# First layer's moba queries computed with queries along the free axis, in four accumulators, with the rotary step on GpSimd

## The chip, the cores and the metric

The kernel runs on one core of one Trainium2 chip. The time is device microseconds of one execution of the whole program; smaller is better. The core's engines run side by side, each through its own instructions in order: TensorE (PE in the profile; PEld is its weight load), VectorE (DVE), ScalarE (ACT), GpSimd (POOL), and SyncE (SP), whose queue issues nearly all transfers here.

## The reference, cut to what matters

A decoder trunk of two layers over 256 tokens of width 1024, in float32. Each layer norms `x`, projects it once with `w_in`, runs three token mixers side by side (MLA attention, MoBA attention, retention), gates and merges them, and then runs a squared-ReLU MLP. The change touches the MoBA queries of the first layer:

```python
h = rms_norm(x, attn_norm[l])
p = h @ w_in                      # mq is 512 of its columns: 8 heads x 64
q, k = partial_rope(heads(mq)), partial_rope(heads(mk))   # rotates 16 of each head's 64
s = q @ k.T * 64 ** -0.5          # causal softmax over the 256 keys, then @ v
```

With 256 tokens and blocks of 256 there is one block, so MoBA is plain causal attention here. The norm's factor `r` (one per token) is applied to a projection's result; its gains are multiplied into `x` beforehand.

## The kernel before, in words

**Numbers.** A float32 product is made of three fp32r products. `x` is split into high and low parts (`xs`: `split`, L234; `take`, L255; `take_first`, L260), each weight tile too: `fetch` (L189) makes `whi` by a ScalarE copy (L200) and `wlo` by a VectorE subtraction (L202). Both have six buffers, and the `raw` tiles that the transfers fill have seven (`RAW`, L1219).

**Two ways to project.** "Rows" (L334, and `start`, L684): a 128-token tile of `x` is the stationary operand, up to 512 weight columns move, and the result has tokens on partitions. "Turned" (`project_turned`, L369): 128 weight columns are stationary, both parts of `x` (2 x 256 columns) move in one matmul with `whi` (L378), then the high part (256 columns) moves with `wlo` (L380). One PSUM bank then holds two halves, which are joined: ScalarE copies the second half (L384), VectorE adds the first to it (L385) into `qkraw`. Two such units fill a pair, and `rope_turned` (L400) rotates the pair: four transfers on SP's queue swap 32-partition groups (L406), then a product with cosines (L409), one with sines on GpSimd (L410), and a sum (L411), into a `qkT` tile. The tables that it multiplies with carry the norm's factor (`tables`, L392).

**The first layer's start.** Weights arrive while the work begins, so `start` (L684) goes through the eight 128-row tiles of `w_in` as they land. For each tile it adds to two banks `b0` (MLA's 416 columns, in the pool `misc`) and two banks `mq` (512 MoBA query columns, in the pool `acc`): high parts first (L705, L706), then the weights' low parts (L708). The pools `acc` and `misc` have four banks each (L208, L211). After the last tile `moba_done` (L673) copies the two `mq` banks to SBUF with the norm's factor (L677) and VectorE rotates them by `rope` (L414: L423 to L426). Then `project_turned` makes the keys `mk`, one `acc` bank for each of its four units; `c_norms` (L643) works on `b0` meanwhile. Much later `moba_turn` (L848) transposes the queries on TensorE (L854, eight transposes in two groups of four, 128x128) and ScalarE copies them out (L858). `moba_scores` (L861, matmuls L444) uses them.

**The second layer** makes its queries turned already: four units before those of `mk`, and `moba_rope("mq", i)` at the units 1 and 3 of `mk` (L823), all its products on GpSimd.

**What sets the order.** `prog` lists the units of work in order of TensorE; `at` hangs further steps behind a unit. Inside `manual_schedule` an engine keeps the order of the source. Elsewhere a planner lays down each engine's order before the program runs, with durations of its own (L1297); the source's order is a preference, and an instruction that the planner believes ready may be put ahead of others. On the chip each engine then keeps the planned order, whatever is ready. In the start, ScalarE, VectorE and TensorE keep the source's order up to tile 5 (L1200 to L1202); tiles 6 and 7 and what follows are planned.

Of the kernel before, what the change touches and what calls it, by code (L numbers as in the profile page):

```python
# [7 lines left out]
F32 = mybir.dt.float32  # L8
# [6 lines left out]
P = 128  # L15
D = 1024
S = 256
NT = S // P
# [100 lines left out]
K_MASK = K_ID + P  # L119
K_COS_MLA = K_MASK + 2 * P  # L120
K_SIN_MLA = K_COS_MLA + NT * 32
K_COS_MB = K_SIN_MLA + NT * 32
K_SIN_MB = K_COS_MB + NT * 8
K_DEC = K_SIN_MB + NT * 8

K_TURNED_RT = K_DEC + RT_H * 3 * P
K_TURNED_MB = K_TURNED_RT + 2 * S
# [10 lines left out]
def trunk(ctx: ExitStack, tc: tile.TileContext, gx, wts, consts, gfin, gn, xtok, out):  # L138
# [69 lines left out]
    def acc_tile(name="acc"):  # L208
        return ps.tile([P, 512], F32, name=name, tag="acc", bufs=4)
# [4 lines left out]
    def w2k(name):  # L214
        return sb.tile([P, 512], F32, name=name, tag="w2k", bufs=W2K)
# [12 lines left out]
    def halves(tile_):  # L228
        return tile_.rearrange("p (two s) -> p two s", two=2)
# [132 lines left out]
    def project_t(l, key, n, xn, o):  # L362

        wh, wl = load_w(l, key, n, 0)
        for k in range(KD):
            xh, xl = xn.k(k)
            three(o, wh[:, k, :], wl[:, k, :], xh, xl, k == 0, k == KD - 1)

    def project_turned(l, key, xn, done):  # L369


        pair = []

        def unit(n):
            wh, wl = load_w(l, key, n, 0)
            acc = acc_tile()
            for k in range(KD):
                nc.tensor.matmul(acc, wh[:, k, :], xn.both(k), start=k == 0, stop=False)  # L378
            for k in range(KD):
                nc.tensor.matmul(acc[:, 0:S], wl[:, k, :], xn.k(k)[0], start=False, stop=k == KD - 1)  # L380
            if n % 2 == 0:
                pair.append(w2k("qkraw"))
            second = sb.tile([P, S], F32, name="second", tag="relu", bufs=3)
            nc.scalar.copy(second, acc[:, S : 2 * S])  # L384
            nc.vector.tensor_add(halves(pair[-1])[:, n % 2, :], acc[:, 0:S], second)  # L385
            if n % 2:
                done(n // 2, pair[-1])

        for n in range(4):
            prog.append(((key, n), lambda n=n: unit(n)))  # L390
# [23 lines left out]
    def rope(xv, c0, s0, t, n, h, w=None):  # L414

        w = w or n
        cos = K[:, c0 + t * w : c0 + t * w + n][:, None, None, :].to_broadcast([P, h, 2, n])
        sin = K[:, s0 + t * w : s0 + t * w + n][:, None, None, :].to_broadcast([P, h, 2, n])
        a = sb.tile([P, S], F32, name="ropea", bufs=1)
        b = sb.tile([P, S], F32, name="ropeb", bufs=1)  # L420
        av = a[:, : 2 * h * n].rearrange("p (h two n) -> p h two n", h=h, two=2)
        bv = b[:, : 2 * h * n].rearrange("p (h two n) -> p h two n", h=h, two=2)
        nc.vector.tensor_mul(av, xv, cos)  # L423
        nc.vector.tensor_mul(bv, xv, sin)
        nc.vector.tensor_sub(xv[:, :, 0, :], av[:, :, 0, :], bv[:, :, 1, :])
        nc.vector.tensor_add(xv[:, :, 1, :], av[:, :, 1, :], bv[:, :, 0, :])  # L426
# [209 lines left out]
    def layer(l, xn, before):  # L636
# [36 lines left out]
        def moba_done(key):  # L673
            def done(accs):
                dst = mqkv[key] = [w2k(key) for _ in range(NT)]
                for t in range(NT):
                    nc.scalar.activation(dst[t], accs[t], AF.Copy, scale=xn.col[t])  # L677
                    if key == "mq":
                        xv = dst[t].rearrange("p (h two r) -> p h two r", h=MB_H, two=2)[:, :, :, 0:8]
                        rope(xv, K_COS_MB, K_SIN_MB, t, 8, MB_H)  # L680

            return done

        def start(k, mq):  # L684

            if k == 0:
                b0.extend(misc_tile("b0") for _ in range(NT))
                mq.extend(acc_tile() for _ in range(NT))
            before(k)
            ah, al = xn.k(k)  # L690
            if k == 0:

                blocks = [(mq, slice(0, 256), load_w(l, "mq", 0), 0, True), (mq, slice(256, 512), load_w(l, "mq", 1), 0, False)]
                blocks.append((b0, slice(0, 416), load_w(l, "b0", 0), 0, True))
            else:
                w = load_w(l, "b0mq", k)
                blocks = [(b0, slice(0, 416), w, 0, False), (mq, slice(0, 512), w, 416, False)]

            for part in ("high", "low"):
                for accs, cs, w, c, begins in blocks:  # L700
                    ws = slice(c, c + cs.stop - cs.start)
                    for t in range(NT):
                        o, sl = accs[t][:, cs], slice(P * t, P * t + P)
                        if part == "high":
                            nc.tensor.matmul(o, ah[:, sl], w[0][:, 0, ws], start=begins, stop=False)  # L705
                            nc.tensor.matmul(o, al[:, sl], w[0][:, 0, ws], start=False, stop=False)  # L706
                        else:
                            nc.tensor.matmul(o, ah[:, sl], w[1][:, 0, ws], start=False, stop=k == KD - 1)  # L708
            if k == KD - 1:
                moba_done("mq")(mq)  # L710

        qkT = {"mq": {}, "mk": {}}

# [105 lines left out]
        if l == 0:  # L819
            at(slot("mv", 3), lambda: tc.keep_in_program_order(nc.sync.dma_start(TAB, consts[:, K_TURNED_MB:])))  # L820
        for i in range(2):
            if l:
                at(slot("mk", 1 + 2 * i), lambda i=i: moba_rope("mq", i))  # L823
            at(slot("gmla0", 1 + 2 * i), lambda i=i: moba_rope("mk", i))
        first = slot("mv", 3)
        at(first, lambda: omlaT.extend((t4("omlah"), t4("omlal"))))
# [18 lines left out]
        first = slot("gmoba1", 1)  # L845
        at(first, lambda: omobaT.extend((t4("omobah"), t4("omobal"))))

        def moba_turn(i):  # L848

            pt = misc_tile("pq")  # L850
            for a in range(2):
                for t in range(NT):
                    k = 2 * i + a
                    nc.tensor.transpose(  # L854
                        pt[:, (2 * a + t) * P : (2 * a + t + 1) * P], mqkv["mq"][t][:, P * k : P * k + P], ident
                    )
            o = sb.tile([P, 2 * S], F32, name="qkT", bufs=4)
            nc.scalar.copy(o, pt)  # L858
            qkT["mq"][i] = halves(o)

        def moba_scores(h0):  # L861
            banks = [misc_tile("ps_s") for _ in range(4)][::-1]
            together(
# [2 lines left out]
            )  # L866
            return banks

        if l == 0:
            for i in range(2):  # L870
                at(first + 4 * i - 3, lambda i=i: moba_turn(i))
        moba_last = attention(omobaT, None, lambda: mqkv["mv"], MB_D**-0.5, first, moba_scores, mla_last)


# [347 lines left out]
def constants():  # L1222

    import numpy as np

    f = np.float32
    K = np.zeros((P, K_END), f)
    i = np.arange(P)
    K[:, K_ID : K_ID + P] = np.eye(P, dtype=f)
    K[:, K_MASK + P : K_MASK + 2 * P] = np.where(i[None, :] <= i[:, None], 0.0, NEG_INF)  # L1230
    for h in range(RT_H):
        lg = np.log(1.0 - 2.0 ** (-5.0 - h))
        diff = np.arange(S)[None, :] - i[:, None]
        dec = np.where(diff >= 0, np.exp(lg * np.maximum(diff, 0)), 0.0) * RT_K**-0.5
        K[:, K_DEC + 384 * h : K_DEC + 384 * h + S] = dec
        K[:, K_DEC + 384 * h + S : K_DEC + 384 * h + 384] = dec[:, :P]
    def angles(dim, theta):
        inv = f(1.0) / (f(theta) ** (np.arange(0, dim, 2, dtype=f) / f(dim)))
        return np.arange(S, dtype=f)[:, None] * inv[None, :].astype(f)

    for c, s, dim, theta, two in ((K_COS_MLA, K_SIN_MLA, ROPE, 500000.0, 2), (K_COS_MB, K_SIN_MB, MB_D // 4, 500000.0, 1)):
        ang = angles(dim, theta)
        w = two * dim // 2
        for t in range(NT):
            K[:, c + t * w : c + t * w + w] = np.tile(np.cos(ang[P * t : P * t + P]), two)
            K[:, s + t * w : s + t * w + w] = np.tile(np.sin(ang[P * t : P * t + P]), two)
# [54 lines left out]
```

## Time and profile before

| | |
|---|---|
| median of 3 runs | 837.75 us (837.54 to 838.25) |
| the profiled execution: time | 838.08 us |
| the profiled execution: span, first to last instruction | 836.3 us |
| mean granted TensorE clock | 0.998 |
| bytes moved by transfers | 155.23 MB, mean 186 GB/s |

The profile's times count from the start of the span; 1.8 us of the execution lie outside it. In a timeline's row stand the start, the time from the first to the last instruction of the row, engine, source line, operation, tiles (out<-in), shape and count; a bracket at the end gives the idle time before it and what ended it. Matmuls overlap in their recorded durations, so the distance between starts is what a matmul costs.

### The profile page before, as it was taken

Reading aid. Unit: us, or ns where it says so; the run is one execution under the profiler, and the core shown is the slowest. Engines: PE = TensorE matmul, PEld = TensorE weight load, DVE = VectorE, ACT = ScalarE, POOL = GpSimd, SP = SyncE. Lnnn points to the kernel's source line nnn. Section 1 sums busy time; section 2 is a strip of 40 time slices with the busy share of each in tenths; the row PEclk is TensorE's granted clock in tenths of the full one; section 3 lists DMA queues with packets and bytes.
Section 4 is the critical chain, followed back from the end, with each engine's and each line's share of the span. In section 5 each row is a group of like instructions: output and inputs, shape, how many; then the busy total and the mean of one; then the engine's idle time right before and its main releaser. Section 6 shows DMA issues by size and latency. Waiting matters only on the chain.

```text
span 836.3 us, 12164 instructions
## 1 busy us (share of the span) xinstructions
PE 827.3 (99%) x4382; PEld 702.6 (84%) x4382; DVE 587.7 (70%) x1069; ACT 483.8 (58%) x860; POOL 92.7 (11%) x82
## 2 busy tenths in 40 slices
PE   9999999999999999999999999999999999999997
PEld 7888878888888888888889887888888888888886
DVE  6987667595787666665699975766868775556663
ACT  7767665445556555555676575663555555555552
POOL 0321100040030000000037210002201200000000
PEclk9999999999999999999999999999999999999999
DMA  9966644646457656565465667456565656666611
GB/s 340 359 189 203 213 141 141 197 131 221 141 186 226 184 195 191 189 196 167 133 231 175 190 189 237 154 141 181 157 200 164 213 176 194 198 194 187 196 55 50
DMA packets 45324, 155.23 MB, mean 186 GB/s; under 512 B 5584, under 2 KB 6608, under 8 KB 45008
## 3 DMA queue, kind: packets, MB, share of 16 engines
q1 hardware_dynamic: 44688, 153.79, 58.4%
q8 instruction: 34, 0.56, 0.3%
q10 hardware_dynamic: 576, 0.67, 0.2%
q14 instruction: 26, 0.21, 0.1%
HBM read 150.77 MB, written 1.05 MB: 182 GB/s over the span
## 4 chain that ended last, share of the span: by engine, by line
PE 94%; DMA 2%; DVE 2%; SPq 1%; ACT 0%; POOL 0%; issue 0%; POOLq 0%; DVEq 0%
PE acc L221 17%; PE acc L223 17%; PE acc L222 17%; PE pup L1069 13%; PE pup L1071 7%; PE acc L1019 5%; PE acc L378 4%; PE acc L380 2%; PE ps_s L829 1%; PE ps_pt L478 1%; DMA raw<-wts 1%; DMA qkoth<-qkraw 1%; DVE wlo L202 1%; PE po L505 1%; PE ps_s L444 1%; SPq L406 1%
## 5 line engine op out<-in xcount | busy, mean ns | idle before, releaser
L202 DVE TENSOR_TENSOR wlo<-raw,whi 128x1024 fp32r<-128x1024 f32 (+4 forms) x287 | 343.6, 1204 | 183.2 <-ACT whi L200 130.0
L200 ACT ACTIVATE whi<-raw 128x1024 fp32r<-128x1024 f32 (+4 forms) x287 | 292.3, 1024 | 192.9 <-PE acc L223 115.2
L1069 PE MATMUL pup<-xs,whi 128*128 128x512 f32 x496 | 121.5, 390 | 0.0
L221 PE MATMUL acc<-whi,xs 128*128 128x512 f32 (+1 forms) x304 | 120.2, 395 | 0.0
L223 PE MATMUL acc<-whi,xs 128*128 128x512 f32 (+1 forms) x304 | 118.5, 391 | 0.4 <-DVE xs L237 0.4
L222 PE MATMUL acc<-wlo,xs 128*128 128x512 f32 (+1 forms) x304 | 118.8, 391 | 0.0
L1069 PEld LDWEIGHTS pup<-xs,whi 128*128 128x128 f32 x496 | 91.9, 188 | 18.3
L221 PE MATMUL acc<-whi,sq 128*128 128x512 f32 x256 | 100.1, 391 | 0.0
L222 PE MATMUL acc<-wlo,sq 128*128 128x512 f32 x256 | 99.9, 390 | 0.0
L223 PE MATMUL acc<-whi,sq 128*128 128x512 f32 x256 | 98.8, 389 | 0.0
L1071 PE MATMUL pup<-xs,wlo 128*128 128x256 f32 x496 | 68.8, 283 | 0.0
L1071 PEld LDWEIGHTS pup<-xs,wlo 128*128 128x128 f32 x496 | 65.7, 191 | 3.1
L223 PEld LDWEIGHTS acc<-whi,xs 128*128 128x128 f32 x304 | 57.1, 188 | 12.4 <-DVE xs L237 0.7
L221 PEld LDWEIGHTS acc<-whi,xs 128*128 128x128 f32 x304 | 57.1, 188 | 11.5 <-issue 0.7
L222 PEld LDWEIGHTS acc<-wlo,xs 128*128 128x128 f32 x304 | 57.2, 188 | 10.7
L1080 ACT ACTIVATE relu<-relu 128x256 f32<-128x256 f32 x64 | 25.6, 410 | 54.3 <-DVE relu L1079 54.3
L223 PEld LDWEIGHTS acc<-whi,sq 128*128 128x128 f32 x256 | 48.1, 188 | 10.2
L221 PEld LDWEIGHTS acc<-whi,sq 128*128 128x128 f32 x256 | 48.2, 188 | 9.2
L222 PEld LDWEIGHTS acc<-wlo,sq 128*128 128x128 f32 x256 | 48.2, 188 | 9.0
L273 POOL TENSOR_TENSOR sqsum<-sqsum,xsq 128x256 f32<-128x256 f32 x21 | 23.3, 1111 | 290.7 <-issue 172.4
L378 PE MATMUL acc<-xs,whi 128*128 128x512 f32 x160 | 41.3, 395 | 0.7 <-DVE qkraw L385 0.7
L467 ACT ACTIVATE prob<-prob,smx 128x128 f32<-128x128 f32 x64 | 28.4, 445 | 18.3 <-DVE smx L464 18.3
(243 smaller groups left out, 1153.4 us busy)
## 6 DMA issues: line engine op xcount, KB each, us to landing
raw<-wts SPq DMA_DIRECT2D x264, 512.0 KB, 4.2
raw<-wts SPq DMA_DIRECT2D x6, 464.0 KB, 8.5
qkoth<-qkraw SPq DMA_DIRECT2D x40, 64.0 KB, 4.5
dec<-consts SPq DMA_DIRECT2D x2, 1024.0 KB, 4.8
raw<-wts SPq DMA_DIRECT2D x4, 416.0 KB, 3.2
xrow<-xtok SPq DMA_DIRECT2D x4, 256.0 KB, 8.0
gn<-gn SPq DMA_DIRECT2D x2, 512.0 KB, 5.4
raw<-wts SPq DMA_DIRECT2D x3, 256.0 KB, 3.7
```

Source lines behind the costliest of these rows:

```text
L200: nc.scalar.activation(hi[:, cs], raw[:, cs], AF.Copy)
L202: nc.vector.tensor_sub(lo[:, cs], raw[:, cs], hi[:, cs].bitcast(F32))
L221: nc.tensor.matmul(o, ah, bh, start=start, stop=False)
L222: nc.tensor.matmul(o, ah, bl, start=False, stop=False)
L223: nc.tensor.matmul(o, al, bh, start=False, stop=stop)
L273: (nc.gpsimd if n < self.on_pool else nc.vector).tensor_add(self.sum, self.sum, sq)
L378: nc.tensor.matmul(acc, wh[:, k, :], xn.both(k), start=k == 0, stop=False)
L467: nc.scalar.activation(p[:, a:b], p[:, a:b], AF.Exp, bias=m[:, 2 + i : 3 + i], scale=scale, accum_out=m[:, 4 + i : 5 + i])
L1019: nc.tensor.matmul(o, a, b, start=half == 0 and i == 0, stop=4 * half + n == KD and i == len(jobs) - 1)
L1069: nc.tensor.matmul(u, w, xm.both(k), start=k == 0, stop=False)
L1071: nc.tensor.matmul(u[:, 0:S], w, xm.k(k)[0], start=False, stop=k == KD - 1)
L1080: nc.scalar.activation(s, s, AF.Square)
```

## The change

In the first layer the queries are made turned too. `start` keeps four `acc` banks instead of two. For each weight tile, and each group n of 128 query columns, it issues one matmul with `whi` over both parts of `x` (512 moving columns) and one with `wlo` over the high part (256). At tile 0 the queries come ahead of `b0` in each part, at tiles 1 to 6 behind it. At the last tile the order is: both parts of group 0, all of `b0`, then groups 1, 2 and 3. The four joins follow, by a helper `joins` that was cut out of `project_turned`. `moba_rope("mq", i)` now runs in the first layer too, behind the units 0 and 2 of `gmla1`; its three products of 512 columns each run on GpSimd, its eight transfers on SP's queue. `moba_turn`, the copies with the norm's factor and the VectorE rotation of the queries are gone, and with them the tables that they used (32 of 544 columns of the `K` transfer, L609).

```diff
+    def joins(done):
+        pair = []
+        def join(n, acc):
+            if n % 2 == 0:
+                pair.append(w2k("qkraw"))
+            second = sb.tile([P, S], F32, name="second", tag="relu", bufs=3)
+            nc.scalar.copy(second, acc[:, S : 2 * S])
+            nc.vector.tensor_add(halves(pair[-1])[:, n % 2, :], acc[:, 0:S], second)
+            if n % 2:
+                done(n // 2, pair[-1])
+        return join
...
-                    if key == "mq":
-                        xv = dst[t].rearrange("p (h two r) -> p h two r", h=MB_H, two=2)[:, :, :, 0:8]
-                        rope(xv, K_COS_MB, K_SIN_MB, t, 8, MB_H)
...
-                mq.extend(acc_tile() for _ in range(NT))
+                mq.extend(acc_tile() for _ in range(4))
...
+            def turned_part(part, ns):
+                for n in ns:
+                    if part == 0:
+                        nc.tensor.matmul(mq[n], wq[n][0], xn.both(k), start=k == 0, stop=False)
+                    else:
+                        nc.tensor.matmul(mq[n][:, 0:S], wq[n][1], ah, start=False, stop=k == KD - 1)
...
+            if k < KD - 1:
+                for part in range(2):
+                    for job in (turned_part, b0_part) if k == 0 else (b0_part, turned_part):
+                        job(part, range(4)) if job is turned_part else job(part)
+            else:
+                join = joins(moba_pair("mq"))
+                for part in range(2):
+                    turned_part(part, [0])
+                for part in range(2):
+                    b0_part(part)
+                for n in range(1, 4):
+                    for part in range(2):
+                        turned_part(part, [n])
+                for n in range(4):
+                    join(n, mq[n])
...
-            if l:
-                at(slot("mk", 1 + 2 * i), lambda i=i: moba_rope("mq", i))
+            at(slot("mk", 1 + 2 * i) if l else slot("gmla1", 2 * i), lambda i=i: moba_rope("mq", i))
...
-        def moba_turn(i):
...
-        if l == 0:
-            for i in range(2):
-                at(first + 4 * i - 3, lambda i=i: moba_turn(i))
```

More of the change, by code (lines that the diff above doesn't have):

```diff
@@ L121 @@
 K_SIN_MLA = K_COS_MLA + NT * 32
-K_COS_MB = K_SIN_MLA + NT * 32
-K_SIN_MB = K_COS_MB + NT * 8
-K_DEC = K_SIN_MB + NT * 8
+K_DEC = K_SIN_MLA + NT * 32
 K_TURNED_RT = K_DEC + RT_H * 3 * P
@@ L367, in project_t @@
             three(o, wh[:, k, :], wl[:, k, :], xh, xl, k == 0, k == KD - 1)
+    def joins(done):
[9 more added lines that the diff above has]
+        return join
     def project_turned(l, key, xn, done):
-        pair = []
+        join = joins(done)
         def unit(n):
@@ L380, in unit @@
                 nc.tensor.matmul(acc[:, 0:S], wl[:, k, :], xn.k(k)[0], start=False, stop=k == KD - 1)
[L381 to L387, printed above, removed]
+            join(n, acc)
         for n in range(4):
@@ L691, in start @@
             if k == 0:
-                blocks = [(mq, slice(0, 256), load_w(l, "mq", 0), 0, True), (mq, slice(256, 512), load_w(l, "mq", 1), 0, False)]
-                blocks.append((b0, slice(0, 416), load_w(l, "b0", 0), 0, True))
+                ws = [load_w(l, "mq", i) for i in range(2)]
+                wq = [[w[:, 0, P * i : P * i + P] for w in two] for two in ws for i in range(2)]
+                wb = [w[:, 0, :] for w in load_w(l, "b0", 0)]
             else:
                 w = load_w(l, "b0mq", k)
-                blocks = [(b0, slice(0, 416), w, 0, False), (mq, slice(0, 512), w, 416, False)]
@@ L699, in start @@
[L699 to L708, printed above, removed]
@@ L709, in start @@
-            if k == KD - 1:
-                moba_done("mq")(mq)
+                wq = [[part[:, 0, 416 + P * n : 416 + P * n + P] for part in w] for n in range(4)]
+                wb = [part[:, 0, 0:416] for part in w]
+            def turned_part(part, ns):
[4 more added lines that the diff above has]
+                        nc.tensor.matmul(mq[n][:, 0:S], wq[n][1], ah, start=False, stop=k == KD - 1)
@@ new lines, in b0_part @@
+            def b0_part(part):
+                for t in range(NT):
+                    o, sl = b0[t][:, :416], slice(P * t, P * t + P)
+                    if part == 0:
+                        nc.tensor.matmul(o, ah[:, sl], wb[0], start=k == 0, stop=False)
+                        nc.tensor.matmul(o, al[:, sl], wb[0], start=False, stop=False)
+                    else:
+                        nc.tensor.matmul(o, ah[:, sl], wb[1], start=False, stop=k == KD - 1)
+            if k < KD - 1:
+                for part in range(2):
+                    for job in (turned_part, b0_part) if k == 0 else (b0_part, turned_part):
+                        job(part, range(4)) if job is turned_part else job(part)
+            else:
+                join = joins(moba_pair("mq"))
[8 more added lines that the diff above has]
+                    join(n, mq[n])
@@ L846, in layer @@
         at(first, lambda: omobaT.extend((t4("omobah"), t4("omobal"))))
-        def moba_turn(i):
[L850 to L859, printed above, removed]
         def moba_scores(h0):
@@ L1239, in angles @@
         return np.arange(S, dtype=f)[:, None] * inv[None, :].astype(f)
[L1241 to L1246, printed above, removed]
+    ang, w = angles(ROPE, 500000.0), ROPE
+    for t in range(NT):
+        K[:, K_COS_MLA + t * w : K_COS_MLA + t * w + w] = np.tile(np.cos(ang[P * t : P * t + P]), 2)
+        K[:, K_SIN_MLA + t * w : K_SIN_MLA + t * w + w] = np.tile(np.sin(ang[P * t : P * t + P]), 2)
     for j, (dim, theta) in enumerate(((RT_K, 10000.0), (MB_D // 4, 500000.0))):
```

## The prediction

> **What bounds the kernel now.** I read the page's busy times first, then the list of waits of TensorE, then timelines of the two places that the change touches: the first 41 us, and the stretch from 101 to 116 us where the removed transposes ran.
>
> ```profile
> PE 827.3 (99%) x4382; PEld 702.6 (84%) x4382; DVE 587.7 (70%) x1069; ACT 483.8 (58%) x860; POOL 92.7 (11%) x82
> ```
>
> ```profile
> PE warm L616 <- PEq L1294: 0.8, 1, 0.8
> PE acc L378 <- DVE qkraw L385: 0.7, 1, 0.7
> PE b L705 <- ACT whi L200: 0.6, 1, 0.6
> PE ps_r L444 <- DVE qkT L411: 0.5, 1, 0.5
> PE acc L223 <- DVE xs L237: 0.4, 1, 0.4
> ```
>
> TensorE has work in 827.3 of 836.3 us. Its waits sum to 3.0 us, 0.8 of them ahead of its first instruction; most of the other 6 us lie behind its last matmul. So an instruction taken from TensorE is worth what it occupies there, work taken from another engine is worth nothing by itself, and any new wait of TensorE is paid in full. No wait of the list belongs to the first layer's queries: the whole gain must come from TensorE's own instructions.
>
> **What goes: eight transposes.** The timeline of TensorE around both groups; transposes of the other attention (L478) stand between those of the first group, and what a matmul costs is the distance to the next start.
>
> ```profile
> 102.29 0.27 PE L478 MATMUL ps_pt<-K,prob 128*128 128x128 f32 x1
> ...
> 102.97 0.47 PE L223 MATMUL acc<-whi,xs 128*128 128x512 f32 x1
> ```
>
> ```profile
> 114.68 0.60 PE L854 MATMUL pq<-K,mq 128*128 128x128 f32 x4
> 115.03 0.48 PE L221 MATMUL acc<-whi,omlah 128*128 128x512 f32 x1
> 115.35 0.40 PE L222 MATMUL acc<-wlo,omlah 128*128 128x512 f32 x1
> ```
>
> Between 102.29 and 102.97 run seven transposes, three L478 and four L854, so 0.68 / 7 = 0.097 us each: the four are worth 0.39 us. The second group takes 115.03 - 114.68 = 0.35 us, and the 512-column matmul behind it 0.32 us where the next section measures 0.23 in a steady row: 0.09 us more. Sum: **0.83 us** off the path. The two copies L858 that follow were ScalarE work beside TensorE's: nothing.
>
> **What moves: the query matmuls of the start.** Columns per weight tile stay 3072. Two stretches of the timeline give the price of each form, the old one in tile 3, the new one in the first layer's `mk`.
>
> ```profile
> 16.16 0.40 PE L705 MATMUL acc<-whi,xs 128*128 128x512 f32 x1
> ...
> 17.10 0.54 PE L708 MATMUL b<-wlo,xs 128*128 128x416 f32 x2
> 17.47 0.63 PE L708 MATMUL acc<-wlo,xs 128*128 128x512 f32 x2
> 17.94 0.35 PE L705 MATMUL b<-whi,xs 128*128 128x416 f32 x1
> ```
>
> ```profile
> 28.52 2.00 PE L378 MATMUL acc<-xs,whi 128*128 128x512 f32 x8
> 30.36 1.12 PE L380 MATMUL acc<-xs,wlo 128*128 128x256 f32 x8
> 31.31 2.00 PE L378 MATMUL acc<-xs,whi 128*128 128x512 f32 x8
> ```
>
> Old: four high matmuls in 17.10 - 16.16 = 0.94, two low ones in 17.94 - 17.47 = 0.47, together 1.41 us per tile. New: a 512-column matmul costs (30.36 - 28.52) / 8 = 0.23, a 256-column one (31.31 - 30.36) / 8 = 0.119; four of each are 1.40 us. Two instructions more per tile cost nothing. I count **0**, with 0.1 us either way over eight tiles.
>
> The very beginning: the first new matmul reads both parts of `x`, the first old one only the high part.
>
> ```profile
> 4.14 0.38 PE L705 MATMUL acc<-whi,xs 128*128 128x256 f32 x1
> 4.43 0.39 PE L706 MATMUL acc<-whi,xs 128*128 128x256 f32 x1
> ...
> 5.37 0.35 PE L705 MATMUL b<-whi,xs 128*128 128x416 f32 x1
> ...
> 10.28 0.46 PE L705 MATMUL b<-whi,xs 128*128 128x416 f32 x1 [0.62 <-ACT whi L200]
> ```
>
> The first to read the low part started at 4.43. From there four matmuls of 0.23 end at 5.35, where `b0` starts now too (5.37). A delay of some tenths would vanish in the 0.62 us that TensorE waits for tile 2 at 10.28, whose transfer the change leaves alone. **0**; without that cover it would be at most 4.43 - 4.14 = 0.29.
>
> **What is added on the path: a wait for a bank.** Before, the start left two of the four `acc` banks free, so `mk` could begin without a copy. Now it holds all four, and the first `mk` unit must wait until group 0 has been joined: a ScalarE copy of 256 columns (L384) and a VectorE addition (L385). All three engines around the end of the start, then the first join after it:
>
> ```profile
> 22.81 1.06 ACT L200 ACTIVATE whi<-raw 128x1024 fp32r<-128x1024 f32 x1 [1.23 <-DMA raw<-wts]
> ...
> 22.98 0.35 PE L705 MATMUL b<-whi,xs 128*128 128x416 f32 x1
> ...
> 23.90 4.29 DVE L202 TENSOR_TENSOR wlo<-raw,whi 128x1024 fp32r<-128x1024 f32 x4 [1.07 <-ACT whi L200]
> ...
> 24.03 1.06 ACT L200 ACTIVATE whi<-raw 128x1024 fp32r<-128x1024 f32 x1 [0.17 <-DMA raw<-wts]
> ...
> 25.26 1.58 ACT L200 ACTIVATE whi<-raw 128x1024 fp32r<-128x1024 f32 x2 [0.17 <-PE b L708]
> ...
> 25.64 2.09 PE L378 MATMUL acc<-xs,whi 128*128 128x512 f32 x8
> 26.75 0.67 ACT L677 ACTIVATE mq<-acc,ms 128x512 f32<-128x512 f32 x1
> ...
> 31.43 0.39 ACT L384 COPY second<-acc 128x256 f32<-128x256 f32 x1
> ...
> 33.10 0.41 DVE L385 TENSOR_TENSOR qkraw<-acc,second 128x256 f32<-128x256 f32 x1
> ```
>
> The last tile starts at 22.98. Group 0 runs first there and takes 0.23 + 0.119 = 0.35, so it is done at 23.33; TensorE wants the bank at 25.64. The cover is **2.31 us**, against 0.39 + 0.41 us of work and two handovers. But ScalarE and VectorE are in a row of weight splits just then, held back by transfers (1.23 us of idle ahead of 22.81), and what they do next was laid down by the planner, not by what is ready. The old query copy shows it: its bank was complete by 25.5, and it ran at 26.75, behind the pair of splits from 25.26. What the join takes from TensorE's end to the addition's end I bound by two rows. The first `mk` group ends at 28.52 and its addition at 33.10 + 0.41 = 33.51: 4.99 us, which would make TensorE wait 4.99 - 2.31 = 2.68. The nearer one is the same event in the second layer, a bank of `mq` that the fourth unit needs:
>
> ```profile
> 430.66 0.86 PE L378 MATMUL acc<-xs,whi 128*128 128x512 f32 x3
> ...
> 433.54 2.11 PE L378 MATMUL acc<-xs,whi 128*128 128x512 f32 x8 [0.74 <-DVE qkraw L385]
> ```
>
> There the group ended at 430.66 and the bank was usable at 433.54, 2.88 us later; that would be a wait of 0.57. Laid on the start's own rows: if the copy stands behind the split of 24.03, it ends near 25.4; if the addition then stands behind the second of four subtractions (23.90 + 2 x 1.07 = 26.05), it ends at 26.46 and TensorE goes on near 26.6, a wait of 1.0. I take **1.0**, between 0.57 and 2.68 and nearer the former, and keep 0 and 3.0 as the ends. Queued behind the waiting matmul are all of `mk` and everything later on TensorE, so nothing hides it. The other three joins follow within some tenths, and their banks are wanted 2.8 us apart (28.52, 31.31).
>
> **What is added off the path.** GpSimd gets six products, SP eight transfers. The queries are due at the first MoBA scores:
>
> ```profile
> 109.47 1.51 PE ps_s L444 x16
> ```
>
> ```profile
> 99.74 2.42 POOL L397 TENSOR_TENSOR tab<-dec,rrow 128x256 f32<-128x256 f32 x2 [23.28 <-DMA dec<-consts]
> ```
>
> GpSimd sits idle for 23.28 us ahead of 99.74, just where the two rotations fall; six products of 1.3 to 2.2 us fit, and retention's tables at 99.74, which reuse the table buffer, lose nothing. Without that idle time the scores would have 9.7 us left. On SP a rotation's four transfers took about 2.4 us of issuing in the keys' case, ahead of weight loads that run several tiles in front. The second layer does all of this already, and the list of waits has none of TensorE on a transfer, a weight split or a MoBA rotation there. **0**. VectorE swaps eight small rotation operations for four additions, ScalarE two copies L677 of 0.67 and two L858 for four copies of 0.39: no chain of TensorE hangs on either.
>
> One row speaks against GpSimd as the place:
>
> ```profile
> 38.55 1.30 POOL L409 TENSOR_TENSOR qkT<-qkraw,tab 128x512 f32<-128x512 f32 x1
> 38.61 2.33 DVE L202 TENSOR_TENSOR wlo<-raw,whi 128x1024 fp32r<-128x1024 f32 x1
> ```
>
> A subtraction that takes 1.07 in the row of four takes 2.33 beside that product: VectorE loses up to 1.3 us for each. [...]
>
> **Sum.** -0.83 + 0 + 0 + 1.0 = +0.17 us. On the profiled execution (838.08, of which 836.3 are span) that is 838.25; on the median of the runs shown, which lies 0.33 lower, **837.9**.
>
> **Rivals.**
> *The bank is free in time.* The planner puts the copy and the addition ahead of the split of 24.03 and its subtraction. For it: ScalarE idles at 22.8 for lack of weights, and 0.8 us of work has 2.31 us. Against: none of the joins named above was that quick. It gives 837.75 - 0.83 = 836.9.
> *The join lands behind the whole row of splits* (the other side). The planner may believe the weights there earlier than the transfers bring them. Then the copy runs where L677 runs now (26.75 to 27.1), the addition behind the fourth subtraction (23.90 + 4.29 = 28.19, so to 28.6), and TensorE waits 3.0: 837.75 - 0.83 + 3.0 = 839.9. Two splits less give 1.9 and 838.8. It decides from 2.5 us of wait on, which is the copy behind the pair of 25.26.
> *GpSimd's products slow VectorE where it is full.* The first products of the queries need only tables and raw queries, and may be put near 38 to 46 us, ahead of the first scores of MLA. Two of them cost VectorE 2.6 us; if half comes through, 837.9 + 1.3 = 839.2. Against: the second layer shows no such wait with as many products.
> *The change does not do what it says:* the planner, which orders tiles 6 and 7, draws `b0` or another group ahead of group 0. Then the cover shrinks by up to 1.1 us and the wait grows by that: 839.0.
>
> **How the numbers follow.** A measurement of this kernel can tell about 0.2% from no change, 1.68 us, so 836.1 to 839.4 counts as the same. Chances: forecast (wait 0.3 to 1.5) 0.35; free in time 0.27; a wait of 1.5 to 2.4 0.11; behind the whole row 0.19; GpSimd 0.05; not as it says 0.03. Slower are the whole row (0.19), and parts of the last two and of unforeseen orders later in the layer: 0.27. Nothing in the sum reaches -1.68; 0.03 for faster is left for a reordering that removes one of the waits listed. The range goes from the free bank (836.9, 0.1 lower for the matmuls) to the whole row (839.9, 0.1 higher).
>
> **What would show it.** L854 gone, and 0.83 us gained by 116 us against the start of `mk`; the tile distance of 2.52 us in the start unchanged; a wait of L378 on L385 near 25.6 in the list of TensorE's waits, its length the term I am least sure of; no wait of L444 or L478 between 60 and 110. I am wrong if that wait is absent or near 3, or if a new wait stands in the first layer's attention.

## The result, and the profile after

| | before | after |
|---|---|---|
| median | 838.0 us (837.32 to 838.68) | 841.16 us (839.5 to 842.77) |
| ratio | | 1.004, 95% interval 1.003 to 1.005 |
| the profiled execution: time, span, mean clock | 838.08 us, 836.3 us, 0.998 | 840.05 us, 838.2 us, 0.999 |

The forecast was 837.9, in a range from 836.8 to 840.0. The changed kernel is 3.2 us slower by the medians and 2.0 by the profiled executions; the two are explained apart below. (`project_turned`'s matmuls are now L391 and L393, the join L375 and L376, the splits L198 and L200, the queries of the start L707 and L709.)

The page's busy times, then the list of TensorE's waits over the whole span (total, times, longest):

```profile
PE 826.3 (99%) x4384; PEld 702.5 (84%) x4384; DVE 592.8 (71%) x1065; ACT 482.2 (58%) x860; POOL 101.3 (12%) x88
```

```profile
PE acc L391 <- DVE qkraw L376: 3.5, 2, 2.7
PE warm L623 <- PEq L1301: 0.8, 1, 0.8
PE acc L707 <- DVE xs L262: 0.7, 1, 0.7
PE ps_r L451 <- DVE qkT L418: 0.6, 1, 0.6
PE acc L221 <- DVE xs L235: 0.4, 1, 0.4
```

TensorE does 1.0 us less and waits more. The new wait stands in the first row: of its 3.5 us in two places, 2.7 are the first key unit in the first layer (the other is the old one in the second layer). L707 waiting 0.7 us for `xs` at the very beginning takes the place of the 0.6 that `b0` waited for tile 2. The timeline around the new wait:

```profile
20.46 1.06 ACT L198 ACTIVATE whi<-raw 128x1024 fp32r<-128x1024 f32 x1 [0.52 <-DMA raw<-wts]
23.01 1.06 ACT L198 ACTIVATE whi<-raw 128x1024 fp32r<-128x1024 f32 x1 [1.49 <-DMA raw<-wts]
24.29 1.06 ACT L198 ACTIVATE whi<-raw 128x1024 fp32r<-128x1024 f32 x1 [0.22 <-DMA raw<-wts]
25.57 1.06 ACT L198 ACTIVATE whi<-raw 128x1024 fp32r<-128x1024 f32 x1 [0.22 <-DMA raw<-wts]
26.53 0.35 ACT L375 COPY second<-acc 128x256 f32<-128x256 f32 x1
```

```profile
23.04 0.35 PE L715 MATMUL b<-whi,xs 128*128 128x416 f32 x1
...
24.10 3.78 DVE L200 TENSOR_TENSOR wlo<-raw,whi 128x1024 fp32r<-128x1024 f32 x3 [1.32 <-ACT whi L198]
...
25.21 0.38 PE L329 MATMUL pss<-K,ms 128*128 128x128 f32 x2
...
27.80 0.42 DVE L376 TENSOR_TENSOR qkraw<-acc,second 128x256 f32<-128x256 f32 x1
...
28.27 0.50 PE L391 MATMUL acc<-xs,whi 128*128 128x512 f32 x1 [2.68 <-DVE qkraw L376]
```

Group 0 is done at 23.04, where `b0` starts. ScalarE is idle then (1.49 us ahead of 23.01), but its next three instructions are splits of key weights, each of which starts when its transfer lands. The copy comes behind them at 26.53, the addition behind three subtractions at 27.80. The keys start at 28.27 where they started at 25.64. Of these 2.63 us the removed transposes give back most of a microsecond; at the first layer's retention scores the kernel before stands at

```profile
155.46 1.58 PE L444 MATMUL ps_r<-qkT 64*128 64x256 f32 x16
```

and the changed kernel at

```profile
157.12 1.14 PE L451 MATMUL ps_r<-qkT 64*128 64x256 f32 x10
```

that is 1.66 us later at the scores, and 1.9 at the end of the span.

That is the profiled execution. Of all 13 executions of the changed kernel, four lie at 839.33 to 840.05 with a mean granted TensorE clock of .999, and nine at 840.83 to 842.82 with .995 to .997. The median is in the second group. What these lose shows in a profile of one of them (842.75 us). First come stretches of that execution: from and to, their length, the busy time of PE, PEld, DVE, ACT and POOL (with the number of instructions), then TensorE's granted clock (1.00 is full), the DMA share and GB/s. Then comes its timeline.

```profile
25.00:27.00 2.00, 0.31 (x3) 0.06 (x1) 1.95 (x2) 1.77 (x2) 0.00 (x0) 1.00 1.02 406
27.00:28.00 1.00, 0.00 (x0) 0.00 (x0) 0.94 (x2) 1.00 (x4) 0.00 (x0) 0.73 1.05 410
28.00:34.00 6.00, 5.20 (x16) 4.43 (x17) 4.67 (x19) 5.12 (x14) 0.00 (x0) 0.50 1.02 404
34.00:35.00 1.00, 1.00 (x6) 0.86 (x5) 0.62 (x1) 0.67 (x3) 0.00 (x0) 0.85 1.03 406
```

```profile
28.80 3.78 PE L391 MATMUL acc<-xs,whi 128*128 128x512 f32 x8 [3.49 <-DVE qkraw L376]
32.38 1.91 PE L393 MATMUL acc<-xs,wlo 128*128 128x256 f32 x8
34.09 2.12 PE L391 MATMUL acc<-xs,whi 128*128 128x512 f32 x8
```

By the stretches the clock falls to half at 28.00 - 2 x 0.27 = 27.46, while TensorE waits, and stays there until 34.00 + 2 x 0.15 = 34.3. The first key unit takes 34.09 - 28.80 = 5.29 us; another execution of the same kernel (839.93 us), with full clock, shows

```profile
28.25 2.11 PE L391 MATMUL acc<-xs,whi 128*128 128x512 f32 x8 [2.01 <-DVE qkraw L376]
30.20 1.11 PE L393 MATMUL acc<-xs,wlo 128*128 128x256 f32 x8
31.15 2.00 PE L391 MATMUL acc<-xs,whi 128*128 128x512 f32 x8
```

2.90 us. The loss is 2.4 us in the one unit. The start is 0.55 later besides, and that lateness is older than the fall of the clock: from 24 to 26, at a clock of 1.00 in both, VectorE is busy for 1.33 us, in the other execution for 1.86. Together that is 2.9, against 842.75 - 839.93 = 2.8.

### The profile page after: what moved, and what is told of

It is laid out like the page before. It is cut to its first block, busy times and chain, and to the rows that moved or that the text cites. A ratio compares the mean times of both kernels' runs of the same rounds, so it can differ in the third digit from the quotient of the medians.

```text
span 838.2 us, 12188 instructions
## 1 busy us (share of the span) xinstructions
PE 826.3 (99%) x4384; PEld 702.5 (84%) x4384; DVE 592.8 (71%) x1065; ACT 482.2 (58%) x860; POOL 101.3 (12%) x88
## 4 chain that ended last, share of the span: by engine, by line
PE 93%; DMA 3%; DVE 2%; ACT 0%; issue 0%; SPq 0%; POOL 0%; DVEq 0%; POOLq 0%; ACTq 0%
PE acc L219 17%; PE acc L221 17%; PE acc L220 17%; PE pup L1078 13%; PE pup L1080 7%; PE acc L1028 5%; PE acc L391 4%; PE acc L393 2%; DMA raw<-wts 2%; PE ps_s L854 1%; PE ps_pt L485 1%; DMA xrow<-xtok 1%; PE po L512 1%; DVE wlo L200 1%; PE ps_s L451 1%; DMA qkoth<-qkraw 1%
## 5 line engine op out<-in xcount | busy, mean ns | idle before, releaser
L200 DVE TENSOR_TENSOR wlo<-raw,whi 128x1024 fp32r<-128x1024 f32 (+4 forms) x287 | 345.1, 1210 | 180.7 <-ACT whi L198 127.6
L198 ACT ACTIVATE whi<-raw 128x1024 fp32r<-128x1024 f32 (+4 forms) x287 | 291.9, 1023 | 189.4 <-PE acc L221 106.1
L1089 ACT ACTIVATE relu<-relu 128x256 f32<-128x256 f32 x64 | 25.5, 408 | 54.4 <-DVE relu L1088 54.4
L221 PEld LDWEIGHTS acc<-whi,sq 128*128 128x128 f32 x256 | 48.1, 188 | 10.2
L391 PE MATMUL acc<-xs,whi 128*128 128x512 f32 x160 | 41.4, 395 | 3.5 <-DVE qkraw L376 3.5
```

Of the source, the lines that this page charges most:

```text
L198: nc.scalar.activation(hi[:, cs], raw[:, cs], AF.Copy)
L200: nc.vector.tensor_sub(lo[:, cs], raw[:, cs], hi[:, cs].bitcast(F32))
L221: nc.tensor.matmul(o, al, bh, start=False, stop=stop)
L1089: nc.scalar.activation(s, s, AF.Square)
```

## The experiments: the wait

Theory W: the loss is the wait of the first key unit for its bank, and the gain is the transposes. Theory G: GpSimd's products and SP's transfers cost something of their own. Theory C: the pause also costs clock. The kernel before was timed again beside each of four sets of kernels: 837.53 us in the first, 837.40 in the second, 837.44 in the third, 837.37 in the fourth. In the cuts of code, ... stands for lines left out.

**The removed work alone** (the kernel before, without the transposes):

```diff
-                at(first + 4 * i - 3, lambda i=i: moba_turn(i))
+                at(first + 4 * i - 3, lambda i=i: qkT["mq"].__setitem__(i, qkT["mk"][i]))
```

> The kernel before, without moba_turn: the first layer's MoBA scores use the turned keys in the place of the queries, so that the eight transposes and their two copies are left out, and nothing else. It measures the gain term by itself: 0.83 us less than before by the sum of its rows, 837.2 beside 838.0. If the transposes were hidden or the planner's order moved with them, the time would stay within 0.3 us of before.

Measured 836.47, ratio 0.9987 (0.9978 to 0.9996): a gain of 1.06 us, by the interval 0.33 to 1.84, with the 0.83 of the sum inside. That term of the sum stands.

**Another bank for group 0** (the changed kernel):

```diff
-                mq.extend(acc_tile() for _ in range(4))
+                mq.extend([misc_tile("mq0"), *(acc_tile() for _ in range(3))])
```

> The changed kernel with query group 0 in a bank of the other pool, so that mk's first unit finds a free bank in acc; the planned order of copies and splits is left as it comes. Theory W: mk's first unit begins near 25.4 without a wait, but the second wants the bank of group 1 near 28.2, and that join ends near 29.1 in the changed kernel: a wait of about 1 us there, time near 838.0. If the bank were not the matter but the engines' lateness as such, mk's first unit would still wait 2 us or more, and the time would stay near 840. Theory C: a pause of 1 us costs no clock, spread about 1 us.

Measured 838.14, ratio 1.0009 (1.0000 to 1.0018). The first key unit starts without a wait; the second waits, and longer than expected:

```profile
25.01 2.10 PE L391 MATMUL acc<-xs,whi 128*128 128x512 f32 x8
26.95 1.11 PE L393 MATMUL acc<-xs,wlo 128*128 128x256 f32 x8
29.70 2.12 PE L391 MATMUL acc<-xs,whi 128*128 128x512 f32 x8 [1.65 <-DVE qkraw L376]
```

1.65 - 0.83 = +0.8 against +0.6 measured. No execution has a mean clock under .998.

**Another bank for two groups**, the row of factors (`stats_row`, which needs a bank too) moved behind the second key unit:

```diff
...
+                mq.extend([*(misc_tile("mqm") for _ in range(2)), *(acc_tile() for _ in range(2))])
...
-            at(slot("start", KD - 1), xn.stats_row)
+            at(slot("mk", 1), xn.stats_row)
```

> The changed kernel with groups 0 and 1 of the turned queries in two of the other four banks, and the row of factors made behind the second key unit, so that the first two key units find free banks; the order on ScalarE and VectorE stays as it was apart from that row. Theory W (the wait for the bank, 2.68 us, is the loss, and the eight transposes of 0.83 us are the gain): no wait ahead of the first two key units; the third starts some 5.4 us later than the first wait ended, behind all joins, so 837.53 - 0.83 + 0.1 for the 0.1 us by which the pause of the first tile grew = 836.8, range 836.3 to 837.5. Theory G (the six products on GpSimd or the eight transfers cost in the first layer by themselves): 838 or more though no wait stands ahead of a key unit. Theory C (the pause also costs clock): no pause, so no execution 1.5 us over the others.

Measured 837.11, ratio 0.9995 (0.9986 to 1.0004); a mean clock of .998 or .999 in all eleven executions. The list of TensorE's waits has lost the first layer's keys:

```profile
PE warm L623 <- PEq L1302: 0.8, 1, 0.8
PE acc L391 <- DVE qkraw L376: 0.7, 1, 0.7
PE ps_r L451 <- DVE qkT L418: 0.5, 1, 0.5
PE acc L221 <- DVE xs L235: 0.4, 1, 0.4
PE mqm L707 <- DVE xs L262: 0.3, 1, 0.3
```

(The 0.7 us of L391 is the old wait in the second layer.) With the banks free the whole loss is gone, with GpSimd's products and the transfers still there. So the wait, with what hangs on it, carries the loss. What is left of the gain, 0.3 us, can't be told from nothing nor from the 0.8 of the sum. This is the best version found that computes all of the reference.

**The joins in front of the splits** (the changed kernel; the first join pinned ahead of the second key unit's split, the others ahead of the fourth's, on ScalarE and VectorE):

```diff
...
+            if key in ((0, "mk", 1, 0), (0, "mk", 3, 0)):
+                for ins in joined[key[2] // 3 * 3]:
+                    behind.enter_context(tc.issue_after(ins))
...
```

> The changed kernel with one thing different: on ScalarE and VectorE, the join of query group 0 stands ahead of the split of the second mk tile, and the joins of groups 1 to 3 ahead of the split of the fourth. All work is the same. Theory W (the loss is the wait for the bank, 2.68 us in the profiled execution, because the join stands behind four weight splits that the transfers bring late): the wait of L391 near 25 us goes, mk begins near 25.4, and the time is that of before less 0.83, near 837.2. Theory G (part of the loss is GpSimd's six products and SP's eight transfers in the first layer): the wait goes but the time stays at 838 or more, since those are all still there. Theory C (the pause of TensorE also costs clock in some executions, which is why they spread over 839.5 to 842.8): with the pause gone, the executions lie within about 1 us of each other and all show a clock of 0.998 or 0.999.

Measured 839.12, ratio 1.0017 (1.0008 to 1.0026), where theory W had 837.2. The wait is gone (the keys start at 25.40), since the join now comes when group 0 is done:

```profile
23.28 0.37 ACT L379 COPY second<-acc 128x256 f32<-128x256 f32 x1 [1.79 <-PE acc L714]
23.55 2.01 ACT L202 ACTIVATE whi<-raw 128x1024 fp32r<-128x1024 f32 x2
```

But two others came: MLA's rotated queries `qr` are late at 55.28, and the retention scores of the second layer wait for a split.

```profile
PE pqr L835 <- DVE qr L438: 1.2, 1, 1.2
PE ps_r L456 <- ACT whi L202: 1.1, 1, 1.1
```

All eleven executions have a mean clock of .998 or more, as theory C had it for a kernel without the pause.

**A quarter of the `xrow` transfers**, which run ahead of the key weights:

```diff
...
-        nc.sync.dma_start(xrows[q], xtok[:, q // 2, 512 * (q % 2) : 512 * (q % 2) + 512])
+        nc.sync.dma_start(xrows[q][:, 0:128], xtok[:, q // 2, 512 * (q % 2) : 512 * (q % 2) + 128])
```

> The changed kernel with a quarter of each of the four xrow transfers, and the squares taken over that quarter alone (768 of 1024 columns of each token are left out of the norm's sum). The transfers ahead of mk's weights are 0.77 MB smaller, 1.9 us at the 410 GB/s of that stretch. Theory W: the splits of mk come 1.9 us earlier, the join with them, and the wait falls from 2.7 to about 1 us; time near 838. If instead ScalarE and VectorE themselves were the limit, the wait would fall by no more than the shorter squares, 4 x 0.3 us of ScalarE, and the time would stay near 840.

The norm's sum leaves out 768 of 1024 columns of each token here. Measured 840.38, ratio 1.0025 (1.0014 to 1.0037). The wait fell to 1.80 us only; the start of the keys moved from 28.27 to 28.00. It settles nothing about the transfers: the planner laid the joins further back, three copies in a row behind the short split too, and that took up the time saved. Its use is another: four executions stand at 840.2 to 840.7 with a mean clock of .996 or .997 and two at 838.06 and 838.27 with .998 and .999, and the profiled one is of the first kind (its clock is read in the last section).

## The experiments: GpSimd

**The joins in front, queries unrotated:**

```diff
-            at(slot("mk", 1 + 2 * i) if l else slot("gmla1", 2 * i), lambda i=i: moba_rope("mq", i))
+            if l:
+                at(slot("mk", 1 + 2 * i), lambda i=i: moba_rope("mq", i))
+            else:
+                at(slot("gmla1", 2 * i), lambda i=i: qkT["mq"].__setitem__(i, halves(mqkv["mq", i])))
```

> The variant with the joins in front, with the first layer's queries left unrotated: no six products on GpSimd and no eight transfers in that layer for them. Theory G (its new waits, 1.2 us for VectorE's rotation of MLA's queries and 1.1 us for a split at the retention scores, come of GpSimd's products slowing VectorE): both waits go, 839.1 - 2.0 = 837.1. Rival (the order pinned on ScalarE and VectorE makes the waits, with the products or without): 839.1 within 0.4 us.

Measured 837.06, ratio 0.9996 (0.9987 to 1.0005), where the pinned order alone as the cause would have left 839.1: both waits are gone. Three GpSimd products, in the variant with the joins in front, and a pair of VectorE's subtractions that begins beside them:

```profile
41.29 3.85 POOL L421 TENSOR_TENSOR qkT<-qkraw,tab 128x512 f32<-128x512 f32 x3
```

```profile
43.90 3.45 DVE L204 TENSOR_TENSOR wlo<-raw,whi 128x1024 fp32r<-128x1024 f32 x2
```

and with the queries' products left out:

```profile
43.44 2.35 DVE L204 TENSOR_TENSOR wlo<-raw,whi 128x1024 fp32r<-128x1024 f32 x2
```

The pair takes 1.1 us longer with the products. At the end of it, and at `qr`, VectorE is 1.6 us behind (`qr` is ready at 55.23, without the products at 53.66), where TensorE waited 1.2. The second wait went too, but that is in the second layer, and the planner laid this kernel anew; the rows don't tie it to the products.

**The two other banks, queries unrotated** (the same edit on the best version):

> The variant with two groups in the other banks (837.11), with the first layer's queries left unrotated: no six products on GpSimd and no eight transfers in that layer for them. If the products and transfers cost nothing where VectorE is on time, as the prediction has it: 837.1 within 0.3. Theory G (they cost wherever they stand, as in the variant with the joins in front, where leaving them out gave 2.06): 836.3 or less.

Measured 836.77, ratio 0.9995 (0.9986 to 1.0003), against the same 0.9995 with the rotation. The median lies 0.34 under that of the best version, at the edge of what was expected, and the intervals would not show a cost of that size. So in the best version, where `qr` is ready at 48.1, the products cost nothing that can be told from noise. In the variant with the joins in front it is ready at 55.2, and there they cost TensorE the wait of 1.2 us.

## The experiments: the clock

A pause by hand in the kernel before, nothing of the change in it (the number of powers is what differs):

```diff
...
+            if l == 0 and k == KD - 1:
+                h = small("held")
+                nc.gpsimd.tensor_tensor(h[:, 0:2], w[1][:, 0, 0:2].bitcast(F32), zf[:, 0:2], op=ALU.mult)
+                nc.gpsimd.tensor_tensor(h[:, 0:2], h[:, 0:2], ones[:, 0:2], op=ALU.add)
+                for _ in range(8):
+                    nc.gpsimd.tensor_tensor(h[:, 0:2], h[:, 0:2], neghalf[:, 0:2], op=ALU.pow)
+                held.append(h[:, 0:2])
...
+            if (l, key, n) == (0, "mk", 0):
+                nc.tensor.matmul(acc[:, 0:2], ident, held[0], start=True, stop=True)
```

Eight powers:

> The kernel before, with a pause put by hand ahead of the first key unit: a matmul of two columns into its bank waits for a chain of ten operations of 128x2 on GpSimd (eight of them some 0.71 us each), started by the last split of the first stretch; nothing of the change is in it. The pause should be some 2.7 us, as in the changed kernel. Theory W alone (a pause costs itself): all executions within 0.7 us of 837.53 + 2.7 = 840.2. [...]

Six:

> The same pause by hand with two operations fewer on GpSimd, so some 1.3 us. Theory W alone: 837.53 + 1.3 = 838.8, all within 0.7 us. [...]

Five:

> The kernel before with the pause by hand, one operation of GpSimd fewer than the last (five powers, some 1.14 us each): a pause of some 1.65 us. [...]

Five, and two additions:

> Two additions of 0.27 us more in the chain: a pause of some 2.2 us. [...] Theory W alone: all at 839.6.

A power took 1.24 us in the chain of eight and 1.14 in that of six (9.91 / 8, 6.84 / 6), not 0.71, and the pauses came out longer than planned or shorter. The medians with eight powers, six, and five with two additions (845.58, 842.24, 843.60) lie 5.4, 3.4 and 4.0 above what theory W had put there for the planned pauses, that with five (840.99) 1.9 above 837.44 + 1.65 = 839.09, a pause of the planned length:

| powers | pause in the profiled execution | executions, us (mean clock); the profiled one first |
|---|---|---|
| 8 | 6.08 us | 846.41 (.993); 843.52 (.996), 844.75 (.994), 846.41 (.995) |
| 6 | 2.81 us | 842.24 (.997); 840.54 (.998), 842.23 (.997), 842.74 (.996), 844.23 (.995) |
| 5 and two additions | 2.76 us | 842.15 (.997); 843.39, 843.6, 843.75, 844.03 (all .995) |
| 5 | 1.03 us | 839.08 (.998); 840.43 (.999), 840.99 (.997), 841.92 (.996), 842.68 (.996) |

With six powers, 837.4 + 2.81 = 840.2: one execution is near there (840.54, .998), the others are 2 to 4 us above with a lower clock, like those of the changed kernel. In the profiled one

```profile
28.60 0.38 PE L378 MATMUL acc<-held,K 128*128 128x2 f32 x2 [2.81 <-POOL held L706]
28.85 2.98 PE L380 MATMUL acc<-xs,whi 128*128 128x512 f32 x8
31.62 1.80 PE L382 MATMUL acc<-xs,wlo 128*128 128x256 f32 x8
```

```profile
29.00:30.00 1.00, 1.00 (x5) 0.78 (x6) 0.96 (x4) 1.00 (x3) 0.00 (x0) 0.88 0.95 377
30.00:33.00 3.00, 3.00 (x12) 2.61 (x11) 1.85 (x9) 1.76 (x4) 0.00 (x0) 0.50 0.99 364
33.00:34.00 1.00, 1.00 (x7) 0.87 (x7) 0.48 (x1) 1.00 (x6) 0.00 (x0) 0.92 1.03 387
```

the clock is half for 2 x (0.12 + 0.08) + 3 = 3.4 us, from 29.76, after TensorE has resumed at 28.60. So a pause costs clock without any other part of the change: theory C holds (the kernel before, timed beside these, has .998 or more in every execution). The shortest chain shows the loss too: three of its five executions have .997 or less. How long their pauses were isn't known, only that the profiled one (.998) was 1.03.

**The changed kernel again**, and two more single executions:

> The changed kernel itself, for its profile in an execution that loses clock, and for the share of these. Theory C: executions in two groups, at 839.5 to 840.1 (the wait of 2.68 less the transposes) with a mean clock of .999, and the larger at 840.8 to 843 with .997 or less; in a profile of the second group the rows show TensorE's clock at half for some 3.4 us within 5 us behind the wait and the first key unit's matmuls longer than the 2.12 us for eight; elsewhere the two profiles agree. Theory W alone: the clock stays 1.0 there in every profile and the difference comes from some other place.

> The changed kernel itself, for a profile of an execution that loses clock. Theory C: if the time is over 840.6, the clock reads half for some 3.4 us behind the wait and the first key unit's rows are longer there; if it is under, the clock reads full, as in the two profiles so far.

> The same as the look before it, since four executions in six fall in the slower group.

Measured 841.13, ratio 1.0049 (1.0036 to 1.0061): one execution at 839.93 (.999), four at 841.13 to 842.82 (.997). The single ones took 839.33 (.999) and 842.75 (.995); the profile of the latter is the one shown with the result. Theory C had put the two groups there.

**The pause filled with work** (the changed kernel):

```diff
+            if (l, key, n) == (0, "mk", 0):
+                fill = misc_tile("fill")
+                for _ in range(9):
+                    nc.tensor.matmul(
+                        fill, nc.const_aps.tensor(1.0, [P, P], BF16), nc.const_aps.tensor(1.0, [P, 512], BF16), start=True, stop=True
+                    )
```

> The changed kernel with nine matmuls of 512 columns on constants, into the free bank, put between the first stretch and the first key unit, so that TensorE has work through most of its wait of 2.0 to 2.7 us; they wait for nothing, and nobody reads them. The wait for the bank stays as long, since its end is set by the joins. Theory C (what lies between 840.0 and the median of 841.2 is clock lost after the pause): no execution at a mean clock of .997 or less, all at 839.4 to 840.4, median 839.9. Theory W alone, or a cause elsewhere for the slower executions: two groups as before, median 841.1.

Measured 840.32, ratio 1.0033 (1.0021 to 1.0045); six executions from 839.53 to 840.62, all at .998 or .999. That is 0.4 above what theory C expected and 0.8 under theory W alone. The wait is still there, in part behind the filling (one of its nine matmuls has no record):

```profile
25.16 2.13 PE L392 MATMUL fill<-const-bfloat16-1.0 128*128 128x512 bf16 x8
29.00 2.11 PE L397 MATMUL acc<-xs,whi 128*128 128x512 f32 x8 [1.72 <-DVE qkraw L376]
```

The keys start at 29.00, later than in the four profiles of the changed kernel (28.25 to 28.80), and yet work that nobody needs makes the kernel 0.8 us faster by the medians, because it keeps the upper group from arising: none of six executions is under .998, where nine of 13 without the filling are at .997 or less. The idleness is what cost the clock here; the wait as such costs its length.

## Why the prediction was wrong, point by point

- **Transposes, -0.83**: 1.06 (0.33 to 1.84 by the interval) with only them taken out. Right.
- **Query matmuls of the start, 0**: not contradicted, but not resolved to tenths either. The factors' row, which follows the last query matmul, stands at 25.21, 25.86, 25.81 and 24.93 in the four profiles of the changed kernel, at 25.50 before, and at 24.73 to 25.55 in those of the kernel with the pause by hand, which has the old start. In the first profile the wait of 0.7 for the low part of `x` came instead of the 0.62 for tile 2, as the cover would have it; but that 0.62 is no fixed cover, since three of the four profiles with the pause by hand lack it.
- **The wait, 1.0 with ends 0 and 3.0**: the first step that failed; it takes the time from 837.9 to near the upper end of the range. Measured 2.68 in the first profile, 2.01 and 2.08 in two others and 3.49 in the fourth. In the first three the keys start at 28.25 to 28.27 all the same, since the joins behind the transfers set the end of the wait; it is shorter where TensorE arrived later. In the fourth they start at 28.80. Against 25.64 before, the term is 2.6 to 3.2. The copy was laid behind the split of 24.03 and came behind the one after it (the split of 25.57 in the changed kernel); the addition was laid behind the second subtraction and came behind the third. Each step of the row is 1.28 us there, the pace at which the transfers land. The choice of the nearer row (0.57, the second layer's) failed because the splits ahead of that join (kernel before) run back to back,

```profile
428.08 3.15 ACT L200 ACTIVATE whi<-raw 128x1024 fp32r<-128x1024 f32 x3 [0.68 <-PE acc L223]
431.13 0.35 ACT L384 COPY second<-acc 128x256 f32<-128x256 f32 x1
```

  with no transfer among what they wait for. The rows of the place itself, where L677 came at 26.75 although its bank was complete by 25.5, said more. The rival of the whole row, at 839.9 with 0.19, came nearest to what happened, though it put the copy and the addition each behind one more split or subtraction than there were. With full clock the measured delay gives the time: -0.83 + 2.63 = 1.8 against 1.97 between the profiled executions.
- **The missing term**: the second step that failed, and the one that took the median out of the range. The prediction has any new wait of TensorE "paid in full", at its length, and no term for the clock behind it: it puts that at nothing without giving a reason. In nine of 13 executions the pause costs about 2.1 us more (the means of the two groups are 839.70 and 841.83), in part through the later start seen above; the four that kept the clock have a mean inside the range. No rival named it, though the pause that it prices at 1.0 to 3.0 is idle time of TensorE in a stretch that is otherwise full.
- **Products and transfers, 0**: right as far as can be measured. The list of waits of the changed kernel shows none that hangs on them in the first layer, and the version with two other banks has 0.9995 with and without them. That cover is thin: with VectorE late they cost about 1.2 us.
- **The change does what it says**: yes; TensorE's order was as written, group 0 ahead of `b0` in the last tile.

## What to carry to other kernels

An instruction that frees a resource waits for its place in its engine's planned order (here group 0 was done at 23.04, and its copy ran at 26.53): read the row of the place itself, see what each instruction in front waits for, and put the new instruction behind all of them before trusting an analogue from a quieter stage. An added wait of TensorE in a full stretch had two prices here, its length (2.01 to 3.49 us in four profiles) and the lower clock that came with it in nine of 13 executions (about 2.1 us, part of it a later start); before paying that, look for another bank, which here cost nothing (ratio 0.9995) and took the loss away.

## What the runs showed of the hardware

The clock's losses came in multiples of one size. In five profiles the time at half clock was read from stretches, as the length at 0.50 plus twice the shortfall of the stretches at the edges: 3.40 us (six powers), 3.40 (five and two additions), 3.42 (the quarter transfers), 6.84 (the changed kernel, 842.75) and 10.24 (eight powers): one, two and three times 3.41. The stretches of the quarter transfers:

```profile
29.00:30.00 1.00, 1.00 (x4) 0.76 (x4) 1.00 (x3) 1.00 (x4) 0.00 (x0) 0.68 1.10 401
30.00:32.00 2.00, 2.00 (x10) 1.86 (x9) 1.29 (x12) 1.37 (x4) 0.00 (x0) 0.50 0.97 385
32.00:33.00 1.00, 1.00 (x5) 0.86 (x5) 0.53 (x1) 0.75 (x6) 0.00 (x0) 0.61 1.01 393
```

2 x (0.32 + 0.39) + 2 = 3.42. The pause's length alone doesn't decide whether clock is lost: in the kernel with the quarter transfers a pause of 1.80 us (26.20 to 28.00) lost clock,

```profile
28.00 2.67 PE L392 MATMUL acc<-xs,whi 128*128 128x512 f32 x8 [1.80 <-DVE qkraw L377]
```

while 2.68, 2.08 and 2.01 us in three profiles of the changed kernel did not. Nor does the fall stand at one place of the pause: with the quarter transfers the clock fell at 30.00 - 2 x 0.32 = 29.36, 1.36 us after the pause had ended, in the execution of 842.75 us at 27.46, 1.34 us before it ended. What decides it is not shown by these runs, and why the chain of five powers lost clock in three executions of five is open: those pauses were not seen.
